# Attention scores issued one matmul ahead of each maximum, from the two auxiliary PSUM banks, instead of in alternating pairs over two kinds of banks

## The chip, the cores and the metric

The kernel runs on one core of a Trainium2 chip. The metric is the device time of one execution in microseconds (us); lower is better. One execution was also recorded by the hardware profiler, and all rows below come from that recording.

## The reference

Two layers of a decoder trunk over 256 tokens of width 1024. Each layer normalises, projects once, and feeds three mixers: sliding-window attention, a short gated convolution and a recurrent branch; then come a merge, a product-key expert FFN and a gated embedding. The part that matters here is the attention, 16 query heads over 4 key/value heads (a group of 4 query heads for each), 64 wide, in two blocks of 128 queries:

```python
scores = jnp.einsum('bnqhgd,bnkhd->bnhgqk', qb, kb,
                    preferred_element_type=jnp.float32) * (HEAD_DIM ** -0.5)
mask = (diff >= 0) & (diff < WINDOW) & (k_pos >= 0)
scores = jnp.where(mask[None, :, None, None], scores, NEG_INF)
m = jnp.maximum(scores.max(axis=-1, keepdims=True), sink)
e = jnp.exp(scores - m)
probs = e / (e.sum(axis=-1, keepdims=True) + jnp.exp(sink - m))
out = jnp.einsum('bnhgqk,bnkhd->bnqhgd', probs.astype(v.dtype), vb)
```

The first block of queries sees 128 keys, the second 256.

## The kernel before

Activations lie transposed, features on the partitions and the 256 tokens along the free axis. A weight is split into a rounded part and a rest (`split`, lines 152 to 161: ScalarE line 159, VectorE line 160), and each product is three matmuls, lines 184 to 186 in `pair`; 48 of them make one PSUM tile of two output chunks. Weights come as a stream, in the order of their use, and their loads and splits are issued ahead.

In a layer the projections of keys (`k`), queries (`q`) and values (`v`, lines 309 to 311) come first, then the attention (lines 315 to 370), then the convolution branch. That branch starts with three projections, `cx`, `cc` and `cb` (lines 375, 380, 388), 48 matmuls each. They need nothing from the attention, so the scheduler may put them between its instructions. Each engine works off its own list in order; the scheduler fixes that list when the kernel is built: of the instructions that it believes ready it takes the one that stands earliest in the program.

PSUM has three kinds of banks: four `acc`, two `mm` (projections, and half of the scores) and two `aux`.

The attention goes over block `b` (0 or 1) and pair of key/value heads `kt` (0 or 1). In a name such as `a01sc` the first digit is the block, the second the key/value head; `sc` is the score tile. The two heads of a pair lie on partitions 0 to 63 and 64 to 127, so a score matmul uses 64 rows of TensorE's array: the upper or the lower half. Steps:

1. Scores, line 328: for a whole pair of heads first, the two heads in turn, one head's tile in an `mm` bank, the other's in an `aux` bank. In block 0 a tile holds four groups of 128x128; in block 1 a head takes two tiles of two groups of 128x256.
2. Scale, mask and maximum in one VectorE operation for each group, line 343, from PSUM to the tile `e`; small operations on the maxima, lines 346 and 347.
3. Exponentials on ScalarE with their sums, lines 349 and 350; then VectorE divides, lines 351 to 354.
4. Four transposes on TensorE for each head and key block into an `acc` bank (`at`, line 361), copied by ScalarE (`et`, line 363), then the product with the values (`ao`, line 366): 64 columns of the array for each head, the left or the right half.
5. The result is split for the branch projection (`store`, lines 272 and 273).

Of the kernel before, what the change touches and what calls it, by code (L numbers as in the profile page):

```python
# [18 lines left out]
P = 128  # L19
# [79 lines left out]
def trunk_kernel(ctx: ExitStack, tc: tile.TileContext, xT, pT, vecs, wmix, wu, wv, outT, dbg=None, layers=NL):  # L99
    nc = tc.nc  # L100
# [12 lines left out]
    def acc_bank(name, shape=(P, 2, T)):  # L113
        return psum.tile(list(shape), F32, name=name, tag="acc", bufs=4)
# [4 lines left out]
    def aux_bank(name, shape=(P, 2, T)):  # L119
        return psum.tile(list(shape), F32, name=name, tag="aux", bufs=2)  # L120
# [149 lines left out]
    def store(dst, src, n=2):  # L270

        nc.scalar.copy(dst[0], src)
        nc.vector.tensor_sub(dst[1], src, dst[0].bitcast(F32))

    def new_big(name, dt=F32, shape=(P, KT, T)):
        return big.tile(list(shape), dt, name=name, tag="big")
# [4 lines left out]
    def t2(name, shape, dt=F32):  # L281
        return work.tile(list(shape), dt, name=name, tag="t2", bufs=3)
# [5 lines left out]
    def layer(l):  # L288
        V = l * V_LAYER
        st = Stream(l)  # L290
        L = "L%d" % l
# [3 lines left out]
        kT = work.tile([P, 2, T], F32, name=L + "kT", tag="wph")  # L295
        ps = pair(st, x1g, L + "k")
        nc.vector.tensor_mul(kT, ps, rb(r1))
        qT = new_big(L + "qT")
# [17 lines left out]
        for b in range(2):  # L316
            nk = b + 1
            for kt in range(2):
                ee = xp.tile([P, 2, 4, nk * P], F32, name=L + "e%d%d" % (b, kt), tag="x")

                scs = {}
                for half in range(nk):
                    for kv in range(2):
                        scs[kv, half] = (aux_bank if kv else mm_bank)(L + "a%d%dsc%d" % (b, 2 * kt + kv, half), (P, 4 // nk, nk * P))
                    for gg in range(4 // nk):
                        for kv in range(2):
                            r0 = kv * 64
                            nc.tensor.matmul(
                                scs[kv, half][:, gg, :], qT[r0 : r0 + 64, 4 * kt + half * 2 + gg, b * P : (b + 1) * P],
                                kT[r0 : r0 + 64, kt, 0 : nk * P], start=True, stop=True)  # L330
                for kv in (2 * kt, 2 * kt + 1):
                    n = L + "a%d%d" % (b, kv)
                    e = ee[:, kv % 2]
                    mx = small.tile([P, 4], F32, name=n + "m", tag="mx", bufs=4)
                    den = small.tile([P, 4], F32, name=n + "d", tag="den", bufs=4)
                    sk = small.tile([P, 4], F32, name=n + "s", tag="sk", bufs=4)

                    sinks = vec[:, V + V_SINK + 8 * kt : V + V_SINK + 8 * kt + 8].rearrange("p (g two) -> p g two", two=2)[:, :, kv % 2]
                    for half in range(nk):
                        sc = scs[kv % 2, half]  # L340
                        for gg in range(4 // nk):
                            g = half * 2 + gg
                            nc.vector.tensor_tensor_reduce(
                                e[:, g, :], sc[:, gg, :], mask.rearrange("p a k -> p (a k)")[:, (2 - nk) * P :],
                                0.125, sinks[:, g : g + 1], OP.add, OP.max, mx[:, g : g + 1])
                    nc.vector.tensor_sub(sk, sinks, mx)
                    nc.vector.tensor_scalar(mx, mx, -1.0, None, op0=OP.mult)
                    for g in range(4):
                        nc.scalar.activation(e[:, g, :], e[:, g, :], AF.Exp, bias=mx[:, g : g + 1], accum_out=den[:, g : g + 1])
                    nc.scalar.activation(sk, sk, AF.Exp)  # L350
                    nc.vector.tensor_add(den, den, sk)
                    nc.vector.reciprocal(den, den)
                    for g in range(4):
                        nc.vector.tensor_scalar(e[:, g, :], e[:, g, :], den[:, g : g + 1], None, op0=OP.mult)  # L354
                po = acc_bank(L + "ao%d%d" % (b, kt), (P, 4, P))
                for kb in range(nk):
                    ets = []
                    for kv in range(2):
                        pt = acc_bank(L + "at%d%d%d%d" % (b, kt, kv, kb), (P, 4, P))
                        for g in range(4):  # L360
                            nc.tensor.transpose(pt[:, g, :], ee[:, kv, g, kb * P : (kb + 1) * P], ident)  # L361
                        et = t2(L + "et%d%d%d%d" % (b, kt, kv, kb), (P, 4, P))
                        nc.scalar.copy(et, pt)  # L363
                        ets.append(et)
                    for kv in range(2):
                        nc.tensor.matmul(  # L366
                            po[kv * 64 : kv * 64 + 64, :, :], vt[:, kb, (2 * kt + kv) * 64 : (2 * kt + kv) * 64 + 64], ets[kv],
                            start=kb == 0, stop=kb == nk - 1, skip_group_check=True)
                s = slice(b * P, (b + 1) * P)
                store([a[:, 4 * kt : 4 * kt + 4, s] for a in attn], po)  # L370
# [83 lines left out]
        for n, branch in enumerate((attn, conv, rec)):  # L454
            for j in range(0, KT, 2):
                ps = pair(st, x1, L + "mg%d%d" % (n, j))
                g = work.tile([P, 2, T], F32, name=L + "gt%d%d" % (n, j), tag="w2a")
# [273 lines left out]
        for j in range(0, KT, 2):  # L731
            ps = pair(st, x3g, L + "pg%d" % j)
            g = work.tile([P, 2, T], F32, name=L + "pgs%d" % j, tag="w2a")
# [6 lines left out]
    for l in range(layers):  # L740
        layer(l)
# [66 lines left out]
```

## Time and profile before

| | |
|---|---|
| median of 3 runs | 2528.94 us (2527.0 to 2531.62) |
| profiled execution | 2527.01 us, its span 2525.3 us |
| TensorE (PE) busy | 2420.9 us, 96% of the span |
| VectorE (DVE) busy | 1779.0 us, 70% |
| ScalarE (ACT) busy | 1307.7 us, 52% |
| mean granted TensorE clock | 0.984 of full speed |

The span is what the profiler saw between the first and the last instruction; the time holds 1.7 us more around it. A matmul in float32 goes through the array in two passes, and the trace has one record for each pass. Records of neighbouring matmuls overlap, since one starts before the one ahead has drained: the distance between two starts tells the pace, the length of a record does not.

### The profile page before, as it was taken

How to read it: one execution, taken by the hardware profiler on the slowest of the kernel's cores; microseconds unless marked ns; L12 is line 12 of the kernel's file. 1: busy time of each engine (PE TensorE's matmuls, PEld its weight loads, DVE VectorE, ACT ScalarE, POOL GpSimd, SP SyncE). 2: the span in 40 equal slices, each digit the busy share in tenths (PEclk: the TensorE clock that was granted, in tenths of full speed). 3: DMA queues.
4: the chain of work that ended last, by engine and by line, in shares of the span. 5: the costliest groups of instructions: out<-in, count | busy, mean ns of one | idle time of the engine just before them, and what ended most of it. 6: DMA issues, size and time to landing. Idle time of an engine off the chain costs nothing. (4 is left out here: it accounts for less than half of the span.)

```text
span 2525.3 us, 42263 instructions
## 1 busy us (share of the span) xinstructions
PE 2420.9 (96%) x17336; PEld 2244.7 (89%) x17336; DVE 1779.0 (70%) x3100; ACT 1307.7 (52%) x1685; POOL 28.8 (1%) x44
## 2 busy tenths in 40 slices
PE   8999998979999999999999999989799999999997
PEld 7899998968899999988879999988798999999886
DVE  7666869999555555567776668699985555555666
ACT  5556454468444444444654554544674444444444
POOL 0000100000000000000000020000000000000000
PEclk9999999989999999999989999999899999999999
DMA  5355443447765656675424545534577566566752
GB/s 190 117 184 184 173 179 135 165 184 266 254 214 205 217 204 219 211 253 197 167 101 151 184 168 186 181 134 151 191 286 245 203 220 211 200 220 209 254 200 84
DMA packets 129459, 486.02 MB, mean 192 GB/s; under 512 B 7536, under 2 KB 73200, under 8 KB 74864
## 3 DMA queue, kind: packets, MB, share of 16 engines
q1 hardware_dynamic: 128976, 482.90, 54.5%
q8 instruction: 136, 2.23, 0.4%
q14 instruction: 59, 0.48, 0.1%
q10 hardware_dynamic: 288, 0.41, 0.0%
HBM read 448.67 MB, written 34.60 MB: 191 GB/s over the span
## 5 line engine op out<-in xcount | busy, mean ns | idle before, releaser
L663 DVE TENSOR_TENSOR L0wt<-L0act,L0gr 128x256 f32<-128x256 f32 x128 | 53.5, 422 | 3.0 <-DMA L0gr<-L0gd 1.0
L663 DVE TENSOR_TENSOR L1wt<-L1act,L1gr 128x256 f32<-128x256 f32 x128 | 53.5, 422 | 2.7 <-DMA L1gr<-L1gd 0.6
L652 ACT ACTIVATE L1act<-L1ua 128x512 f32<-128x512 f32 x64 | 38.0, 594 | 0.0
L652 ACT ACTIVATE L0act<-L0ua 128x512 f32<-128x512 f32 x64 | 38.0, 593 | 0.0
L488 PE MATMUL L0sc<-vec,L0pqs 128*128 128x128 f32 x64 | 9.5, 296 | 6.7 <-DVE L0pqs L505 6.7
L488 PE MATMUL L1sc<-vec,L1pqs 128*128 128x128 f32 x64 | 9.5, 296 | 6.6 <-DVE L1pqs L505 6.6
L488 PEld LDWEIGHTS L0sc<-vec,L0pqs 128*128 128x128 f32 x64 | 8.6, 209 | 7.0 <-issue 7.0
L488 PEld LDWEIGHTS L1sc<-vec,L1pqs 128*128 128x128 f32 x64 | 8.6, 209 | 7.0 <-issue 7.0
L438 DVE RECIPROCAL L0ru<-L0ru 128x256 f32<-128x256 f32 x8 | 14.0, 1746 | 0.1
L438 DVE RECIPROCAL L1ru<-L1ru 128x256 f32<-128x256 f32 x8 | 14.0, 1744 | 0.1
L379 POOL MEMSET L1pc<- 128x4 f32 x4 | 0.4, 103 | 1133.8 <-DVE L1cy L387 1122.4
L366 PE MATMUL L1ao<-L1et,L1vt 128*64 128x512 f32 x24 | 12.4, 770 | 0.1
L361 PEld LDWEIGHTS L1at<-ident,L1e 128*128 128x128 f32 x48 | 6.6, 167 | 6.5 <-DVE L1e L354 1.8
L366 PE MATMUL L0ao<-L0et,L0vt 128*64 128x512 f32 x24 | 11.0, 657 | 0.1
L361 PEld LDWEIGHTS L0at<-ident,L0e 128*128 128x128 f32 x48 | 6.0, 153 | 5.3 <-DVE L0e L354 1.8
L408 DVE SCALAR_TENSOR_TENSOR L1xr<-L1pr,vec,L1xr 128x256 f32<-128x256 f32 x24 | 10.3, 481 | 0.0
L408 DVE SCALAR_TENSOR_TENSOR L0xr<-L0pr,vec,L0xr 128x256 f32<-128x256 f32 x24 | 10.3, 480 | 0.0
L184 PE MATMUL L0k<-L0n1gh,w_0h 128*128 128x256 f32 x8 | 3.3, 412 | 7.2 <-ACT w_0h L159 7.2
L628 PE MATMUL L1t1pg<-L1t1og 128*128 128x128 f16 x16 | 2.0, 307 | 8.3 <-DVE L1t1og L613 8.3
L628 PE MATMUL L0t1pg<-L0t1og 128*128 128x128 f16 x16 | 2.0, 309 | 8.3 <-DVE L0t1og L613 8.3
L363 ACT COPY L1et<-L1at 128x512 f32<-128x512 f32 x12 | 6.7, 582 | 6.3 <-PE L1at L361 6.3
L361 PE MATMUL L1at<-ident,L1e 128*128 128x128 f32 x48 | 9.8, 331 | 0.0
(7266 smaller groups left out, 10950.2 us busy)
## 6 DMA issues: line engine op xcount, KB each, us to landing
w<-wmix SPq DMA_DIRECT2D x137, 1024.0 KB, 4.8
L0u<-wu SPq DMA_DIRECT2D x64, 1024.0 KB, 5.0
L0v<-wv SPq DMA_DIRECT2D x64, 1024.0 KB, 4.8
L1u<-wu SPq DMA_DIRECT2D x64, 1024.0 KB, 4.9
L1v<-wv SPq DMA_DIRECT2D x64, 1024.0 KB, 4.8
L0gr<-L0gd SPq DMA_DIRECT2D x16, 1024.0 KB, 5.9
L1gr<-L1gd SPq DMA_DIRECT2D x16, 1024.0 KB, 5.9
L0gd<-L0t0st SPq DMA_DIRECT2D x1, 1024.0 KB, 4.8
```

What stands on the lines that cost most here:

```text
L184: nc.tensor.matmul(out, w[0], xh, start=start, stop=False, **kw)
L361: nc.tensor.transpose(pt[:, g, :], ee[:, kv, g, kb * P : (kb + 1) * P], ident)
L363: nc.scalar.copy(et, pt)
L366: nc.tensor.matmul(po[kv * 64 : kv * 64 + 64, :, :], vt[:, kb, (2 * kt + kv) * 64 : (2 * kt + kv) * 64 + 64], ets[kv], start=kb == 0, stop ...
L379: nc.gpsimd.memset(pc[:, :, 0:2], 0.0)
L408: nc.vector.scalar_tensor_tensor(o, pr[:, c, i : i + T], w[i], o, op0=OP.mult, op1=OP.add)
L438: nc.vector.reciprocal(u[:, c, :], u[:, c, :])
L488: nc.tensor.matmul(sp[:, b, a, :], q[:, a, b * P : (b + 1) * P], keys[:, a, :], start=True, stop=True)
L628: nc.tensor.matmul(pg[:, t, :], oh[:, 2, t4 + t, :], oh[:, i, t4 + t, :], start=i == 0, stop=i == 1)
L652: nc.scalar.activation(acts[i // 4][:, i % 4 * 2 : i % 4 * 2 + 2, :], ps, AF.Gelu_apprx_tanh)
L663: nc.vector.tensor_mul(wt[:, e, :].rearrange("p (g t) -> p g t", t=SG), acts[i // 4][:, o + e, :].rearrange("p (g t) -> p g t", t=SG), gre ...
```

## The change

The block that issued all scores of a pair of heads ahead of the loop over heads is gone. Each score matmul is now written directly before the VectorE operation that reads it, and all score tiles come from the two `aux` banks. Everything behind line 345 is the same, seven lines higher (the maximum stands in line 336, transposes in 354, the product with the values in 359).

```diff
                 ee = xp.tile([P, 2, 4, nk * P], F32, name=L + "e%d%d" % (b, kt), tag="x")
-
-                scs = {}
-                for half in range(nk):
-                    for kv in range(2):
-                        scs[kv, half] = (aux_bank if kv else mm_bank)(L + "a%d%dsc%d" % (b, 2 * kt + kv, half), (P, 4 // nk, nk * P))
-                    for gg in range(4 // nk):
-                        for kv in range(2):
-                            r0 = kv * 64
-                            nc.tensor.matmul(
-                                scs[kv, half][:, gg, :], qT[r0 : r0 + 64, 4 * kt + half * 2 + gg, b * P : (b + 1) * P],
-                                kT[r0 : r0 + 64, kt, 0 : nk * P], start=True, stop=True)
                 for kv in (2 * kt, 2 * kt + 1):
...
                     for half in range(nk):
-                        sc = scs[kv % 2, half]
+                        sc = aux_bank(n + "sc%d" % half, (P, 4 // nk, nk * P))
+                        r0 = kv % 2 * 64
                         for gg in range(4 // nk):
                             g = half * 2 + gg
+                            nc.tensor.matmul(
+                                sc[:, gg, :], qT[r0 : r0 + 64, 4 * kt + g, b * P : (b + 1) * P],
+                                kT[r0 : r0 + 64, kt, 0 : nk * P], start=True, stop=True)
                             nc.vector.tensor_tensor_reduce(
```

The built program holds the same matmuls, transposes and VectorE and ScalarE operations in the same numbers, and outside the stretch from the first score to the end of `cb`, in both layers, every engine has the same list as before. Inside it the lists differ. TensorE in layer 0, from the last matmul of the values on, in the kernel before:

```order
L311 MATMUL L0v<-w_11h,L0n1sl 128x256
L328 MATMUL L0a00sc_549<-L0kT,L0qT 128x128
L328 MATMUL L0a01sc_550<-L0kT,L0qT 128x128
L328 MATMUL L0a00sc_549<-L0kT,L0qT 128x128
L328 MATMUL L0a01sc_550<-L0kT,L0qT 128x128
L328 MATMUL L0a00sc_549<-L0kT,L0qT 128x128
L328 MATMUL L0a01sc_550<-L0kT,L0qT 128x128
```

The same place in the changed kernel:

```order
L311 MATMUL L0v<-w_11h,L0n1sl 128x256
L333 MATMUL L0a00sc_552<-L0kT,L0qT 128x128
L333 MATMUL L0a01sc_577<-L0kT,L0qT 128x128
L184 MATMUL L0cx_866<-L0n1sh,w_12h 128x256
L185 MATMUL L0cx_866<-L0n1sl,w_12h 128x256
L186 MATMUL L0cx_866<-L0n1sh,w_12l 128x256
L333 MATMUL L0a00sc_552<-L0kT,L0qT 128x128
L184 MATMUL L0cx_866<-L0n1sh,w_12h 128x256
L333 MATMUL L0a01sc_577<-L0kT,L0qT 128x128
L185 MATMUL L0cx_866<-L0n1sl,w_12h 128x256
L186 MATMUL L0cx_866<-L0n1sh,w_12l 128x256
L333 MATMUL L0a00sc_552<-L0kT,L0qT 128x128
```

The 16 scores of block 0 stood in one unbroken run, the heads in turn; now all but the first two stand alone, with one to eleven `cx` matmuls between them, 31 in all before the last score of block 0.

Further on TensorE in layer 0, where block 0's first product with the values stands, in the kernel before:

```order
L361 MATMUL L0at_607<-ident,L0e_548 128x128 x4
L366 MATMUL L0ao_599<-L0et_605,L0vt 64x512
L366 MATMUL L0ao_599<-L0et_612,L0vt 64x512
L328 MATMUL L0a12sc_777<-L0kT,L0qT 128x256 x2
L328 MATMUL L0a12sc_783<-L0kT,L0qT 128x256 x2
L328 MATMUL L0a13sc_778<-L0kT,L0qT 128x256
```

and in the changed kernel, with the scores of block 1 (`a10`, `a11`) about it:

```order
L359 MATMUL L0ao_599<-L0et_605,L0vt 64x512
L354 MATMUL L0at_607<-ident,L0e_548 128x128
L185 MATMUL L0cx_866<-L0n1sl,w_13h 128x256
...
L184 MATMUL L0cc_929<-L0n1sh,w_14h 128x256
L333 MATMUL L0a10sc_692<-L0kT,L0qT 128x256
L359 MATMUL L0ao_599<-L0et_612,L0vt 64x512
L185 MATMUL L0cc_929<-L0n1sl,w_14h 128x256
L333 MATMUL L0a10sc_697<-L0kT,L0qT 128x256
L354 MATMUL L0at_670<-ident,L0e_618 128x128 x4
L186 MATMUL L0cc_929<-L0n1sh,w_14l 128x256
L184 MATMUL L0cc_929<-L0n1sh,w_14h 128x256
L333 MATMUL L0a11sc_718<-L0kT,L0qT 128x256
```

The two halves of the first `ao` were neighbours and are apart. The 16 scores of block 1 stood in 6 stretches in a layer, the first of them right behind block 0's run, and stand in 13. Along the whole list of a layer, the part of the array that TensorE uses (all of it, half the rows for a score, half the columns for an `ao`) changed 25 times and changes 71 times, each change between two neighbouring matmuls.

VectorE in layer 0, where the first division of `e` stands in the changed kernel (line 347, which was line 354):

```order
L336 ISA L0e_618,L0a03m<-L0a03sc_647,mask,vec 128x128
L336 ISA L0a03m 128x1
L344 TENSOR_TENSOR L0a00d<-L0a00d,L0a00s 128x4
L340 TENSOR_SCALAR L0a02m<-L0a02m 128x4
L339 TENSOR_TENSOR L0a03s<-vec,L0a03m 128x4
L345 RECIPROCAL L0a00d<-L0a00d 128x4
L340 TENSOR_SCALAR L0a03m<-L0a03m 128x4
L347 TENSOR_SCALAR L0e_548<-L0e_548,L0a00d 128x128 x4
```

As before, it stands behind the last maximum of head 3 (`a03`), so it follows the last score of block 0.

## Rows read from the trace of the kernel before

**Rows 1.** The page's head: the span, and what TensorE was busy of it.
```profile
span 2525.3 us, 42263 instructions
PE 2420.9 (96%) x17336; PEld 2244.7 (89%) x17336; DVE 1779.0 (70%) x3100; ACT 1307.7 (52%) x1685; POOL 28.8 (1%) x44
```

**Rows 2.** Busy time by stretch; columns named in the first row.
```profile
core 0: us, PE busy (x) PEld busy (x) DVE busy (x) ACT busy (x) POOL busy (x), PEclk, DMA share, GB/s
46.06:97.20 51.14, 48.32 (x283) 33.54 (x281) 34.65 (x145) 32.36 (x97) 0.10 (x1) 0.93 0.18 62
1294.30:1348.64 54.34, 51.72 (x283) 35.66 (x282) 34.76 (x145) 32.47 (x97) 0.10 (x1) 0.84 0.16 59
52.88:59.70 6.82, 6.82 (x19) 3.91 (x19) 4.47 (x29) 3.88 (x18) 0.00 (x0) 0.50 0.01 2
1298.74:1308.98 10.24, 10.24 (x28) 5.94 (x26) 7.29 (x49) 6.11 (x28) 0.00 (x0) 0.50 0.01 2
1312.40:1319.22 6.82, 6.82 (x17) 3.20 (x18) 4.18 (x22) 3.12 (x12) 0.00 (x0) 0.50 0.00 0
```

**Rows 3.** Timeline of PE, block 0's scores: start, length, line, out<-in, idle before.
```profile
45.94 0.28 PE L311 MATMUL L0v<-w_11h,L0n1sl 128*128 128x256 f32 x1
46.15 0.37 PE L328 MATMUL L0a00sc<-L0kT,L0qT 64*128 64x128 f32 x1
46.16 0.37 PE L328 MATMUL L0a01sc<-L0kT,L0qT 64*128 64x128 f32 x1
...
47.82 0.27 PE L328 MATMUL L0a02sc<-L0kT,L0qT 64*128 64x128 f32 x1
...
47.93 0.27 PE L328 MATMUL L0a02sc<-L0kT,L0qT 64*128 64x128 f32 x1
...
50.19 0.48 PE L328 MATMUL L0a10sc<-L0kT,L0qT 64*128 64x256 f32 x1 [1.98 <-DVE L0a00m L343]
```

**Rows 4.** Timeline of PE, block 1's scores: in a run, and alone.
```profile
60.35 0.48 PE L328 MATMUL L0a12sc<-L0kT,L0qT 64*128 64x256 f32 x1
...
60.35 1.99 PE L328 MATMUL L0a12sc<-L0kT,L0qT 64*128 64x256 f32 x8
...
62.91 0.48 PE L328 MATMUL L0a13sc<-L0kT,L0qT 64*128 64x256 f32 x1 [0.56 <-DVE L0a11m L343]
...
67.93 0.38 PE L361 MATMUL L0at<-ident,L0e 128*128 128x128 f32 x2
68.25 0.70 PE L328 MATMUL L0a13sc<-L0kT,L0qT 64*128 64x256 f32 x2
68.87 0.39 PE L184 MATMUL L0cx<-L0n1sh,w_12h 128*128 128x256 f32 x1
69.09 0.28 PE L185 MATMUL L0cx<-L0n1sl,w_12h 128*128 128x256 f32 x1
```

**Rows 5.** Timeline of PE, products with the values between projections.
```profile
72.17 1.07 PE L366 MATMUL L0ao<-L0et,L0vt 128*64 128x512 f32 x2
...
76.11 0.28 PE L186 MATMUL L0cx<-L0n1sh,w_13l 128*128 128x256 f32 x1
76.31 1.08 PE L366 MATMUL L0ao<-L0et,L0vt 128*64 128x512 f32 x4
77.32 0.38 PE L184 MATMUL L0cx<-L0n1sh,w_13h 128*128 128x256 f32 x1
77.55 0.28 PE L185 MATMUL L0cx<-L0n1sl,w_13h 128*128 128x256 f32 x1
```

**Rows 6.** Timeline of PE, one transpose between projections.
```profile
78.62 0.28 PE L185 MATMUL L0cx<-L0n1sl,w_13h 128*128 128x256 f32 x1
78.74 0.27 PE L361 MATMUL L0at<-ident,L0e 128*128 128x128 f32 x1
...
78.97 0.28 PE L184 MATMUL L0cx<-L0n1sh,w_13h 128*128 128x256 f32 x1
```

**Rows 7.** Timeline of DVE: the first maximum and the first division.
```profile
48.97 0.34 DVE L343 CUSTOM_DVE_ANT_0 L0e<-L0a00sc,mask,vec 128x128 f32<-128x128 f32 x1
...
54.02 0.87 DVE L354 TENSOR_SCALAR L0e<-L0e,L0a00d 128x128 f32<-128x128 f32 x4
```

## Prediction, written before the changed kernel was run

> **What bounds the kernel now.** I read the head of the page first: TensorE (PE) is busy 96% of the span [rows 1], so time is PE work plus the few stretches in which PE waits or runs slowly. Then the busy time by stretch around the change. From the end of the values to the end of `cb` a layer takes 51.1 us in layer 0 and 54.3 us in layer 1 [rows 2]. The lists of the two layers are alike there; what differs is the clock, granted at 0.93 and 0.84. The last three of those rows show it: at 0.50 of full speed, the lower level of 1.2 GHz, for 6.8 us in layer 0 and for 10.2 + 6.8 us in layer 1. Ahead of the first fall PE had been waiting: 1.98 us, until VectorE had read the first score tile [rows 3]. Another wait for VectorE is 0.56 us [rows 4]. Behind `cb` both versions have one list, and PE is busy throughout there, so what PE gains or loses in these two stages the whole kernel gains or loses, as long as PE remains what ends them.
>
> The stage's 144 projection matmuls, at a start every 0.12 us (78.62 to 78.74) [rows 6], take 17.3 us in both versions. What changes is the price of scores and of products with the values (`ao`), the waits and the clock.
>
> **The change, part by part.** All for one layer and at the full clock, unless said.
>
> *The price of standing alone.* A score uses half the rows of the array, an `ao` half the columns. In a run, passes over 256 columns start every 0.216 us: eight records span 1.99 us, one 0.48 us, and 1.51 over seven steps is 0.216 [rows 4]. A score on its own is dearer. The transpose ahead, which in its run starts 0.11 us after its neighbour (0.38 less 0.27), starts at 68.04 and the score at 68.25, 0.10 late; the two passes take 0.62 us to the next start instead of 0.43, 0.19 late; the next matmul needs 0.22 us instead of 0.12, 0.10 late [rows 4]. Together 0.39 us. An `ao` between projections shows the same: 0.20 instead of 0.12 us ahead of it, 1.01 us where two passes over 512 columns are 0.86 (an estimate, four times 0.216), then 0.23 instead of 0.12 [rows 5]. Together 0.34 us. A transpose between projections, on the whole array, shows no such price: 0.35 us from one projection to the next but one, that is 0.24 and its own 0.11 [rows 6]. I take 0.38 us for each insertion, with 0.34 and 0.39 as the measured ends. A score of 128 columns alone between projections isn't in the trace; its start is: 0.21 us after the matmul ahead instead of 0.12 [rows 3]. Its unknown end I bound by nothing and by 0.39.
>
> The Trainium skill, TensorEngine Tiling (Array Packing), Key Properties, has a rule that speaks against this change: changing the tiling mode, rather than only the tile, drains TensorE, while different tiles of one mode run in parallel. The transpose without a price and the score and the `ao` with one agree with it [rows 4 to 6]; the page gives no figure. By the rule every added change of mode is paid for; if it were only a first score after a wait that is dear, the added insertions would be nearly free and the sum below would come out at 2517 us.
>
> *Block 0's scores.* Before, heads in turn: two heads start 0.01 us apart and a pass follows every 0.11 us for both [rows 3], so 16 scores of two passes take 16 x 0.11 = 1.76 us. After, only the first two stand together (three steps of 0.11 = 0.33 us) and 14 stand alone, 2 x 0.11 = 0.22 us each: 3.08 + 0.33 = 3.41. That is +1.65 us for the lost overlap, and 14 more insertions.
>
> *Block 1's scores.* They overlap nowhere in either list to speak of; six stretches, the first with no switch ahead of it, become 13: 8 more insertions.
>
> *The first `ao`.* Two neighbours run side by side: four passes last 1.08 us [rows 5], two last 1.07. Apart they cost two passes more, 0.86 us, and one more insertion.
>
> So 14 + 8 + 1 = 23 more insertions, which is also what 71 instead of 25 changes of array part give at two an insertion: 23 x 0.38 = 8.7 us. With the lost overlap, 8.7 + 1.65 + 0.86 = **+11.2 us**.
>
> *Waits that go.* The 1.98 us ahead of `a10` and the 0.56 us ahead of `a13` [rows 3, 4] are filled by projections: **-2.5 us**.
>
> *Waits that come.* Each score of block 0 now waits until VectorE has read the score two places before it in that bank. A maximum takes 0.34 us [rows 7]; PE comes back to a bank after two scores of 0.22 + 0.38 and about four projections of 0.12, 1.7 us. So VectorE is done first, and these waits cost nothing. What is queued behind them are the projections. The first division comes later, though: block 0's scores now last 3.41 + 15 x 0.38 + 31 x 0.12 = 12.8 us, so the last is read at about 46.1 + 12.8 + 0.7 = 59.6 (0.37 for the pass to drain [rows 3], 0.34 for the maximum), and the division starts there instead of at 54.0 [rows 7]. Transposes, exponentials of block 1 and the later `ao` slide by some 5.6 us, and who waits is PE. The cover is the 113 projections that are still to come, 13.6 us, spread between the late pieces up to the last `ao`. I take that this hides it, which costs nothing; if the cover were gone it costs up to 5.6 us in each layer.
>
> *The queues.* No DMA is issued within the moved lines. In the stage the weights' loads and splits keep their order, DMA is at 0.16 to 0.18 of its share [rows 2]; I cost that at nothing.
>
> *The clock.* Without the wait of 1.98 us the falls may go. In layer 0 that is worth 6.8 us at half speed, -3.4 us. In layer 1 the 10.2 us more of low clock cost only the 3.2 us by which its stage is longer, since PE waited for others in part of it: 3.4 + 3.2, -6.6 us. Against it: the scores keep half the array busy, and the drained steps none of it, for a stretch of nearly 13 us. Layer 1 fell a second time, at 1312.4 [rows 2], with the same list with which layer 0 kept its clock at that place. I count one low stretch of 6.8 us as likely as not in each layer, so one in the two: +3.4 us, with none and two of layer 1's size in each as the ends.
>
> **Sum.** Layer 0: 11.2 - 2.5 - 3.4 = +5.3. Layer 1: 11.2 - 2.5 - 6.6 = +2.1. With +3.4 for the clock, +10.8 us. On the profiled execution, 2527.01 (its span of 2525.3 and 1.7 around it), that is 2537.8; the median of the runs shown, 2528.94, lies 1.9 higher, which would give 2539.7. I say 2538.
>
> **Rivals.**
>
> *The cover wins (faster).* Insertions cost little between projections, because the next weights are loaded while the last matmul runs. Then the two layers pay 2 x 2.5 us for lost overlap and gain 5.0 us of waits and 10.0 us of low clock: -10, so 2517. For it: PE does have filler now where it stood for 1.98 us. Against it: the isolated score and the isolated `ao`, both beside projections, were dear. It decides from the price of an insertion: 46 x price = 15 - 5 = 10, so below 0.22 us the change is faster. Chance 0.16.
>
> *It evens out.* With a price between 0.11 and 0.33 us and no low clock the sum is within 5 us of before: about 2529. For it: the unknown end of a 128-column score; if only its start of 0.2 us is dear, 14 of the 23 insertions cost half. Chance 0.20.
>
> *The clock stays low (slower still).* Layer 1's 17.1 us of low clock in both layers, now all of it on PE: 8.5 us each, 7.4 + 17 = +24, 2551; a first division 5.6 us late without cover in each layer, 7.4 + 11.2, would give 2546. Chance 0.12.
>
> That the change doesn't do what it says would need the scheduler to leave the pairs together; its list doesn't, so that holds no chance of its own.
>
> **Chances and range.** The forecast holds 0.52; its own range is 2533 (price of 0.34, full clock) to 2546 (two low stretches and some lost cover). Before can be told from after from 0.2%, 5.1 us: below 2523.9 or above 2534.0. Slower 0.52 + 0.12 = 0.64, same 0.20, faster 0.16. The range for 8 in 10 reaches into the even case and just past it, and part of the way to the low clock: 2522 to 2548.
>
> **What would show it.** In the profile after: block 0's 16 scores spread over about 13 us with 31 `cx` matmuls among them, each alone and 0.4 us dearer than its two passes; no idle time of PE ahead of `a10`; the first division near 59.6 us; the stage of layer 0 at 55 to 57 us and of layer 1 about the same, where before they differed by 3.2; the clock at 1.00 in one of them at least. The prediction is wrong if a lone score costs 0.3 us or less beyond its passes, if PE stands waiting in the second half of the stage, or if anything behind `cb` moves.

## The result, and the profile after

The changed kernel is slower: 2540.07 us, the median of 7 runs (2537.59 to 2552.29), beside 2528.07 us for the kernel before in 7 runs on the same chip (2523.73 to 2531.62). The ratio is 1.0051, with a 95% interval of 1.0038 to 1.0064, so the loss, half a per cent, can be told from none. The forecast was 2538 us. Medians leave out executions in the chip's slower state, two of the 15 of before beside e5.

The profiled execution's span is 2535.9 us, 10.6 longer than before's. The page's head, as in [rows 1]:

```profile
span 2535.9 us, 42242 instructions
PE 2436.9 (96%) x17336; PEld 2251.9 (89%) x17336; DVE 1779.9 (70%) x3100; ACT 1307.1 (52%) x1685; POOL 28.8 (1%) x44
```

The matmuls are the same in number and PE was busy with them for 16 us longer, while the span grew by 10.6: waits became busy time. The busy time by stretch shows where, with the columns of [rows 2]. The first two rows are the two layers' stages from the end of the values to the end of `cb`, the third is the only stretch of low clock in them:

```profile
46.13:105.16 59.03, 58.93 (x283) 38.54 (x282) 34.78 (x144) 32.96 (x98) 0.10 (x1) 0.91 0.20 72
1304.70:1359.16 54.46, 54.38 (x282) 35.20 (x281) 34.77 (x144) 32.95 (x98) 0.13 (x1) 1.00 0.22 78
56.63:66.87 10.24, 10.24 (x34) 7.83 (x34) 3.96 (x25) 2.99 (x16) 0.00 (x0) 0.50 0.00 0
```

Against [rows 2], layer 0 pays 7.9 us and layer 1 0.1. PE has 0.1 us of idle time left in each, where it had 2.8 and 2.6. Layer 1 now runs at the full clock throughout, which before did in neither layer's stage. What is left of the 10.6 us, 2.5, arises in layer 0's expert stage, on unchanged lists, where the clock is also at its lower level for longer: 23.9 us in place of 20.5.

The timeline of PE in layer 0, block 0's scores (start, length, line, out<-in), beside [rows 3]:

```profile
46.22 0.37 PE L333 MATMUL L0a00sc<-L0kT,L0qT 64*128 64x128 f32 x1
46.22 0.37 PE L333 MATMUL L0a01sc<-L0kT,L0qT 64*128 64x128 f32 x1
...
48.64 0.28 PE L186 MATMUL L0cx<-L0n1sh,w_12l 128*128 128x256 f32 x1
48.85 0.49 PE L333 MATMUL L0a00sc<-L0kT,L0qT 64*128 64x128 f32 x2
49.26 0.38 PE L184 MATMUL L0cx<-L0n1sh,w_12h 128*128 128x256 f32 x1
49.58 0.48 PE L333 MATMUL L0a01sc<-L0kT,L0qT 64*128 64x128 f32 x2
49.99 0.38 PE L185 MATMUL L0cx<-L0n1sl,w_12h 128*128 128x256 f32 x1
50.22 0.28 PE L186 MATMUL L0cx<-L0n1sh,w_12l 128*128 128x256 f32 x1
...
59.84 0.79 PE L333 MATMUL L0a03sc<-L0kT,L0qT 64*128 64x128 f32 x2
...
78.83 0.48 PE L333 MATMUL L0a12sc<-L0kT,L0qT 64*128 64x256 f32 x1
78.83 0.48 PE L333 MATMUL L0a11sc<-L0kT,L0qT 64*128 64x256 f32 x1
79.15 0.38 PE L333 MATMUL L0a12sc<-L0kT,L0qT 64*128 64x256 f32 x1
79.15 0.38 PE L333 MATMUL L0a11sc<-L0kT,L0qT 64*128 64x256 f32 x1
```

The first two scores still run side by side (46.22 twice). A lone one is read from starts: from the score at 48.85 to the next at 49.58 are 0.73 us, for one score and one projection. At a pace of 0.12 us for the projection and 2 x 0.11 for the two passes, 0.39 us belong to neither. PE counts as busy in them. The last four rows are two scores of block 1 that happen to stand side by side: four passes in the time of two.

In layer 1, at the full clock, block 0's scores run from the first start at 1304.79 to that of `a10` at 1317.74, 13.0 us:

```profile
1304.79 0.37 PE L333 MATMUL L1a00sc<-L1kT,L1qT 64*128 64x128 f32 x1
...
1317.74 1.13 PE L333 MATMUL L1a10sc<-L1kT,L1qT 64*128 64x256 f32 x4
```

Passes and projections make 7.25 of these 12.95 us (the scores' 3.41 us of the prediction, and 32 x 0.12, one of them behind the last score); the rest, over the 15 places where scores stand, is 0.38 us each. So the lone score above is no exception. VectorE's first division of layer 0, the answer to [rows 7]:

```profile
61.37 0.87 DVE L347 TENSOR_SCALAR L0e<-L0e,L0a00d 128x128 f32<-128x128 f32 x4
```

### The profile page after: what moved, and what is told of

It is laid out like the page before. It is cut to its first block, busy times and chain, and to the rows that moved or that the text cites. A ratio compares the mean times of both kernels' runs of the same rounds, so it can differ in the third digit from the quotient of the medians.

```text
span 2535.9 us, 42242 instructions
## 1 busy us (share of the span) xinstructions
PE 2436.9 (96%) x17336; PEld 2251.9 (89%) x17336; DVE 1779.9 (70%) x3100; ACT 1307.1 (52%) x1685; POOL 28.8 (1%) x44
## 5 line engine op out<-in xcount | busy, mean ns | idle before, releaser
L356 ACT COPY L0et<-L0at 128x512 f32<-128x512 f32 x12 | 6.7, 587 | 10.2 <-PE L0at L354 10.2
L356 ACT COPY L1et<-L1at 128x512 f32<-128x512 f32 x12 | 6.7, 587 | 7.3 <-PE L1at L354 7.3
L401 DVE SCALAR_TENSOR_TENSOR L1xr<-L1pr,vec,L1xr 128x256 f32<-128x256 f32 x24 | 10.3, 480 | 0.0
L401 DVE SCALAR_TENSOR_TENSOR L0xr<-L0pr,vec,L0xr 128x256 f32<-128x256 f32 x24 | 10.3, 480 | 0.0
L354 PEld LDWEIGHTS L0at<-ident,L0e 128*128 128x128 f32 x48 | 6.0, 148 | 4.2 <-issue 2.6
```

Source lines behind the costliest of these rows:

```text
L401: nc.vector.scalar_tensor_tensor(o, pr[:, c, i : i + T], w[i], o, op0=OP.mult, op1=OP.add)
```

## Experiments

Nine runs were made: seven edited kernels, and both kernels once more. Theory: a lone score between projections costs what the two changes of the array part cost, 0.39 us. Rivals: what costs is the lost overlap of the two heads; or the waits behind the two banks; or the clock. Stages are compared over a longer stretch, from the first matmul of the values to the first of the merge gate, since every list agrees again there. For before it is, by stretch, layer 0 then layer 1:

```profile
40.30:195.10 154.80, 151.98 (x1146) 137.16 (x1145) 104.05 (x238) 84.34 (x159) 0.73 (x7) 0.98 0.41 143
1288.50:1446.60 158.10, 155.48 (x1147) 139.38 (x1146) 104.21 (x238) 84.45 (x159) 0.73 (x7) 0.95 0.40 140
```

The same for after:

```profile
40.40:203.10 162.70, 162.60 (x1147) 142.16 (x1146) 104.71 (x238) 84.42 (x159) 0.73 (x7) 0.97 0.38 136
1298.90:1457.10 158.20, 158.12 (x1147) 138.90 (x1146) 104.70 (x238) 84.41 (x159) 0.76 (x7) 1.00 0.39 140
```

Low clock in these: 6.8 and 17.1 us before, 10.2 and none after.

**Only the order of the code (e1_mixed_banks).** The new order, with the old two kinds of banks:

```diff
-                        sc = aux_bank(n + "sc%d" % half, (P, 4 // nk, nk * P))
+                        sc = (aux_bank if kv % 2 else mm_bank)(n + "sc%d" % half, (P, 4 // nk, nk * P))
```

Expected:

> The changed kernel with one edit: the score tiles of even heads come from the projections' two banks again, those of odd heads from the auxiliary ones, as in the kernel before; each score still stands directly ahead of its maximum in the code. The list then has no projection among block 0's scores and 27 changes of array part in a layer, before 25, the changed kernel 71. Theory (lone scores among projections pay 0.39 us each for the change of array part, and it is the free projection bank that puts projections there): as before, 2526 to 2531 us, with the idle time ahead of block 1's scores and the low clock back. Rival (it is the writing of each score ahead of its maximum that costs, by VectorE's read standing between two scores): 2536 us or more.

Measured: 2536.52 us, ratio 1.003 [1.0016, 1.0045]. The part on the list came true: with an `mm` bank held by scores no projection stands between block 0's scores. The total missed. PE's waits are back; waits of PE in layer 1's stage (who waits for whom: us in total, times, longest):

```profile
PE L1a03sc L333 <- DVE L1a03m L336: 1.5, 2, 1.1
PE L1a13sc L333 <- DVE L1a11m L336: 0.7, 1, 0.7
PE L1a10sc L333 <- DVE L1a10m L336: 0.6, 1, 0.6
PE L1a11sc L333 <- DVE L1a03m L336: 0.5, 1, 0.5
```

The stages were 162.3 us (20.5 of it at the low clock) and 156.7 (3.4 of it). So the projections between the scores come from the freed `mm` bank, not from the code order. The order by itself is no gain either: the total met the rival's 2536 us, since scores then wait for VectorE with nothing to fill the wait, and layer 0 ran 20.5 us at the low clock.

**The same list, without a change of array part (e2_full_rows).** Keys are stored twice, with zeros in the other head's rows, and each score uses all 128 rows; the list of PE is that of after.

```diff
-        kT = work.tile([P, 2, T], F32, name=L + "kT", tag="wph")
         ps = pair(st, x1g, L + "k")
-        nc.vector.tensor_mul(kT, ps, rb(r1))
+        kz = work.tile([P, 2, 2, T], F32, name=L + "kz", tag="kz", bufs=1)
+        nc.gpsimd.memset(kz, 0.0)
+        for kv in range(2):
+            nc.vector.tensor_mul(kz[kv * 64 : kv * 64 + 64, kv], ps[kv * 64 : kv * 64 + 64], rb(r1)[kv * 64 : kv * 64 + 64])
...
-                                sc[:, gg, :], qT[r0 : r0 + 64, 4 * kt + g, b * P : (b + 1) * P],
-                                kT[r0 : r0 + 64, kt, 0 : nk * P], start=True, stop=True)
+                                sc[:, gg, :], qT[:, 4 * kt + g, b * P : (b + 1) * P],
+                                kz[:, kv % 2, kt, 0 : nk * P], start=True, stop=True)
```

Expected:

> The changed kernel with the same list on every engine but for the keys: they are stored twice, each time with the rows of the other head at zero, so that a score uses all 128 rows of the array with the queries of both heads, and gives the same numbers. A score then isn't another array part than a projection. Theory (the change of array part costs 0.19 us each): 28 lone scores in a layer cost 0.38 less, 10 us less in a layer, and the 5 us of low clock in layer 0 may go: 2515 to 2522 us, faster than before. Rival (the loss is the overlap of the two heads, 5 us, and the low clock, 5 us, and a lone score costs no more than its passes): overlap isn't given back, so 2535 to 2541 us. In the trace a score of 128 columns between projections should take 0.22 us by the theory, 0.61 by the rival.

Measured: the timeline of PE between the first score and the first of block 1, with a place of the same kind as above at 51.41,

```profile
47.78 0.39 PE L334 MATMUL L0a00sc<-L0kz,L0qT 128*128 128x128 f32 x2
...
49.40 0.28 PE L186 MATMUL L0cx<-L0n1sh,w_12l 128*128 128x256 f32 x1
49.55 0.49 PE L334 MATMUL L0a00sc<-L0kz,L0qT 128*128 128x128 f32 x2
49.80 0.37 PE L184 MATMUL L0cx<-L0n1sh,w_12h 128*128 128x256 f32 x1
50.00 0.38 PE L334 MATMUL L0a01sc<-L0kz,L0qT 128*128 128x128 f32 x2
...
51.41 0.38 PE L334 MATMUL L0a00sc<-L0kz,L0qT 128*128 128x128 f32 x2
51.55 0.36 PE L186 MATMUL L0cx<-L0n1sh,w_12l 128*128 128x256 f32 x1
51.75 0.38 PE L334 MATMUL L0a01sc<-L0kz,L0qT 128*128 128x128 f32 x2
...
56.00 1.17 PE L334 MATMUL L0a10sc<-L0kz,L0qT 128*128 128x256 f32 x4
```

and by stretch the two stages, and layer 0 from the first sums of its expert stage (`acc`) to the keys of layer 1:

```profile
42.00:191.90 149.90, 149.82 (x1147) 138.03 (x1146) 104.32 (x238) 84.35 (x159) 1.69 (x8) 1.00 0.42 148
1298.40:1448.30 149.90, 149.82 (x1146) 138.04 (x1145) 104.33 (x238) 84.35 (x159) 0.77 (x7) 1.00 0.41 148
649.20:1265.60 616.40, 614.83 (x3655) 545.11 (x3656) 366.58 (x435) 295.30 (x350) 0.00 (x0) 0.99 0.61 209
```

From the score at 51.41 to the next 0.34 us, that is 0.12 + 0.22 and nothing more. Other scores keep a part of the price: from 49.40 to 50.00 are 0.60 us for one score and two projections, 0.14 more than 0.22 + 0.24. On average over block 0, 8.22 us (47.78 to 56.00) for 16 x 0.22 + 32 x 0.12 = 7.36, it is 0.05 us a score, where after pays 0.38. What this rest is stays open. The stage falls from after's 158.2, at the same full clock, to 149.9. That is 8.3 us, where 10 were expected: beside the rest, 0.9 us in block 0, two overlaps that after still has (46.22 and 78.83 above; 0.22 + 0.43 us) are gone. This is the experiment that settles the price: same order, same banks, same neighbours. The total did not show it: 2533.57 us, ratio 1.0011 [1.0002, 1.0019], because both expert stages, with unchanged lists, came out some 9 us longer (616.4 where before has 607.0; the last section shows what took longer).

**Full rows in the order of before (e3_full_rows_before).** The same keys and scores in before's code: no overlap of heads anywhere, and no price.

```diff
-                                scs[kv, half][:, gg, :], qT[r0 : r0 + 64, 4 * kt + half * 2 + gg, b * P : (b + 1) * P],
-                                kT[r0 : r0 + 64, kt, 0 : nk * P], start=True, stop=True)
+                                scs[kv, half][:, gg, :], qT[:, 4 * kt + half * 2 + gg, b * P : (b + 1) * P],
+                                kz[:, kv, kt, 0 : nk * P], start=True, stop=True)
```

Expected:

> The kernel before with the keys stored twice with zeros, scores over all 128 rows; list as before. It takes the overlap of the two heads alone, and the few changes of array part at the scores. Theory: block 0's scores last 3.5 us instead of 1.8, but the wait for VectorE behind them is as much shorter, since VectorE begins with the first head's tile after it is free of the weight split; 9 changes of array part fewer give 1.7 us in a layer: 2524 to 2528 us, with the idle time ahead of block 1 near 0.3 us. Rival (overlap is what the changed kernel lost): 2531 to 2534 us.

Measured: 152.1 us in both stages, no low clock, PE waiting 1.3 us of it. That is shorter than either of before's, though every overlap is lost; and against what before's stage would be at the full clock (151.4 to 152.6 us by the estimates further down) it is longer by 0.7 us at most. That is a net: the list has nine changes of array part fewer, some 1.7 us by the price, and PE waits 1.3 us in place of 2.6. So by this estimate the lost overlap costs 3.7 us at most, with every overlap gone. After still has some of them and has its waits filled, and yet by the same estimates its stage lies 5.6 to 6.8 us above before's at the full clock: the lost overlap isn't the loss of after by itself. The total, 2536.96 us and 1.0029 [1.0018, 1.004], carries longer expert stages again.

**Runs of one head and half, all in `aux` banks (e4_runs_aux).** The new banks without the lone scores: for each half, the scores of both heads are issued in turn, then all their maxima.

```diff
+                for half in range(nk):
+                    scs = [aux_bank(L + "a%d%dsc%d" % (b, 2 * kt + kv, half), (P, 4 // nk, nk * P)) for kv in range(2)]
+                    for gg in range(4 // nk):
+                        for kv in range(2):
+                            r0 = kv * 64
+                            nc.tensor.matmul(
+                                scs[kv][:, gg, :], qT[r0 : r0 + 64, 4 * kt + half * 2 + gg, b * P : (b + 1) * P],
+                                kT[r0 : r0 + 64, kt, 0 : nk * P], start=True, stop=True)
+                    for kv in range(2):
+                        for gg in range(4 // nk):
...
```

Expected:

> All score tiles from the auxiliary banks as in the changed kernel, but the code issues the scores of both heads' tiles together, in turn, and then their maxima. Block 0's first 8 scores are one run with overlap, then runs of four and, in block 1, of two; 43 changes of array part in a layer instead of 71, projections between the runs. Theory: 28 fewer changes at 0.19 and 0.9 us of overlap are 6 us less in a layer than in the changed kernel, of which 0.9 goes for one more pair of products with the values standing apart: 2526 to 2530 us, and some 4 us less where layer 0 keeps the full clock. Rival (the auxiliary banks alone are the cost, since a head's tile waits for the one before): 2536 us or more, with PE idle ahead of scores.

Measured: 2525.02 us, ratio 0.9986 [0.9977, 0.9995]. The array part changes 43 times in a layer, between before's 25 and after's 71. Layer 0's stage, at the full clock:

```profile
41.30:194.60 153.30, 152.61 (x1146) 136.62 (x1145) 103.56 (x238) 84.33 (x159) 0.73 (x7) 1.00 0.41 145
```

It is 4.9 us shorter than after's at the full clock, with waits of 0.3 us twice; layer 1's is 153.4. So freeing the `mm` bank is worth having as long as the scores stay in runs.

**Full rows with the keys in their old place (e5_full_rows_in_place).** As e2, but the two copies lie in the tile that held the keys and in a small tile that is free at that time; the zeros go to the unused halves alone.

```diff
+        kz = [work.tile([P, 2, T], F32, name=L + "kT", tag="wph"), small.tile([P, 2, T], F32, name=L + "kU", tag="eT", bufs=2)]
+        for kv in range(2):
+            r = slice(kv * 64, kv * 64 + 64)
+            nc.gpsimd.memset(kz[kv][64 - kv * 64 : 128 - kv * 64], 0.0)
+            nc.vector.tensor_mul(kz[kv][r], ps[r], rb(r1)[r])
```

Expected:

> Full-row scores in the changed kernel's order once more, but the two zero-filled copies of the keys lie where the keys and a tile of the later expert stage lay, so that no tile of the kernel moves in SBUF. In the run with full rows before, the attention stages were shorter by 12.8 and 8.3 us than the changed kernel's, yet each expert stage, whose lists are the same, was some 9 us longer. If that came from where the tiles lie, this one keeps the gain: stages of 150 us from the values to the merge against 158 and 163, and 2514 to 2520 us in all, against some 2529 before. If the longer expert stages come from something else in full-row scores, it stays at 2531 to 2537 us.

Measured: 2519.54 us, ratio 0.9959 [0.9944, 0.9973]. It beats both kernels: 11.9 us below before's median in that comparison, 2531.44, and 23.4 below after's there (2542.91, in e7). PE's timeline:

```profile
48.08 0.36 PE L184 MATMUL L0cx<-L0n1sh,w_12h 128*128 128x256 f32 x1
48.28 0.38 PE L335 MATMUL L0a01sc<-L0kU,L0qT 128*128 128x128 f32 x2
48.42 0.36 PE L185 MATMUL L0cx<-L0n1sl,w_12h 128*128 128x256 f32 x1
```

The two stages, and the expert stretch of layer 0 as in e2:

```profile
41.20:191.10 149.90, 149.82 (x1146) 138.02 (x1145) 104.32 (x238) 84.30 (x159) 0.73 (x7) 1.00 0.41 148
1286.50:1436.40 149.90, 149.83 (x1147) 138.03 (x1146) 104.33 (x238) 84.29 (x159) 0.73 (x7) 1.00 0.41 148
646.30:1253.70 607.40, 605.84 (x3656) 543.13 (x3656) 366.12 (x434) 294.90 (x350) 0.52 (x1) 1.00 0.61 212
```

A projection follows 0.14 us behind the score's start (48.28, 48.42), and the next projection 0.20 later: 0.34 for a projection and two passes, as in e2. The expert stretch is back at before's length, so the whole gain of the stages reaches the total.

**A spare tile (e6_spare_tile).** Why were e2's expert stages longer? Before's code with an unused tile of the size of e2's keys:

```diff
+        spare = work.tile([P, 2, 2, T], F32, name=L + "spare", tag="spare", bufs=1)
+        nc.gpsimd.memset(spare, 0.0)
```

Expected:

> The kernel before with one more tile of 4 KB a partition, set to zero on GpSimd and never read, in the pool where the two copies of the keys lay; nothing else changed. If the place of tiles in SBUF made the expert stages of the full-row runs longer, this kernel is slower than before by 10 to 18 us, all of it in the expert stages. If not, it is within 4 us of before.

Measured: 2530.54 us, ratio 0.9997 [0.9986, 1.0007], expert stretch 607.4 us. Shifting the tiles behind it is not the cause by itself. Its stages were 155.5 and 155.2 us, with 10.2 us of low clock in each.

**After once more (e7_after_again).** No edit. Expected:

> The changed kernel as it is, for a second profile beside the same runs of before. Theory: the attention stages at the full clock repeat to 0.3 us (158.2 us from the values to the merge, 59 less 5.1 of clock in layer 0), while the low stretches fall elsewhere: layer 0 or 1 may have one of 3 to 10 us or none. Rival (the low stretch in layer 0 belongs to the list): it is there again with about 10 us in layer 0 and none in layer 1.

Measured: 2542.91 us, ratio 1.0052 [1.0036, 1.0068]. The two stages:

```profile
40.40:203.10 162.70, 162.60 (x1147) 142.18 (x1146) 104.72 (x238) 84.64 (x159) 0.73 (x7) 0.97 0.39 136
1298.90:1461.60 162.70, 162.62 (x1146) 141.84 (x1145) 104.67 (x238) 84.64 (x159) 0.76 (x7) 0.97 0.38 137
```

Layer 0 repeats to the tenth. Layer 1, which ran in 158.2 us at the full clock, now has 10.2 us of low clock too, and takes 162.7. So neither expectation held in full: the low stretch of layer 0 was there again, and layer 1 had one as well. The two profiles of one kernel so give the price of such a stretch here: 4.5 us.

**Before once more (e8_before_again).** No edit. Expected:

> The kernel before as it is, for a second profile. Theory: low clock again in both attention stages, since PE stands for 2 us in each, of 7 to 17 us; the stages last 151 us plus half of the low clock or a little less.

Measured: 2530.93 us; the stages are 154.9 and 158.1 us, with 6.8 and 17.1 us of low clock, as in the first profile.

**Keys and values exchanged (e9_swap_places).** Before's code, with the two tiles' places exchanged:

```diff
-        kT = work.tile([P, 2, T], F32, name=L + "kT", tag="wph")
+        kT = work.tile([P, 2, T], F32, name=L + "kT", tag="wpl")
...
-        vt = work.tile([P, 2, 256], F32, name=L + "vt", tag="wpl")
+        vt = work.tile([P, 2, 256], F32, name=L + "vt", tag="wph")
```

Expected:

> The kernel before with the keys and the values exchanging their tiles' places (one line each); lists and sizes are the same. In the full-row runs whose keys had left their place the expert stages, with unchanged lists, took about 9 us longer; the run with a spare tile did not, nor did the full-row run in which the keys kept their place. If it is the order in which the places of the expert stage's two product tiles are laid out that counts, this kernel is 10 to 18 us slower than before, in the expert stages; if not, it is within 4 us of before and the cause of those 9 us stays open.

Measured: 2528.78 us, ratio 0.9997 [0.9987, 1.0006], expert stretch 607.3 us. The keys' place alone isn't the cause of e2's longer expert stages either.

## Why the prediction was right, and where its sizes were off

**The price of standing alone: right.** Forecast 0.38 us for each insertion; a lone score measured 0.39 us, and 0.05 on average (0.00 at one place, 0.14 at another) when the same scores in the same places use the whole array. The bound that was unknown, a 128-column score alone between projections, lies at its upper end. Of the Trainium skill the rule weighed in the prediction (TensorEngine Tiling (Array Packing), Key Properties) is borne out: these runs show a price of 0.38 us on average where the array part changes, and 0.05 where it doesn't. The same page of the Trainium skill, in its Overview, recommends reconfiguring the array into smaller tiles where the contracted dimension is 64 or less. Here that pays only where two such matmuls are neighbours (46.22 twice): for a lone one, e2 and e5 show the whole array cheaper, 0.22 to 0.36 us for a score instead of 0.61.

**Waits that go: right.** The 2.0 and 0.6 us ahead of `a10` and `a13` are gone in both layers, and by e1 it is the free bank that lets projections fill them.

**Waits that come: right at nothing.** PE has no wait in the stages of after, though the first division came at 61.4 us, later than the 59.6 that were forecast; the low clock from 56.6 on reaches into block 0's last scores. The 113 projections still covered it. In layer 1, at the full clock, block 0's scores took 13.0 us, forecast 12.8, and the first division came 13.4 us behind the first score's start (1318.23), forecast 13.5.

**The sum at the full clock: too large.** After has a measured full-clock stage, 158.2 us. That is 3.4 and 0.1 us above before's two stages, 154.8 and 158.1 with their low clock, where the prediction's sums without new low clock are 5.3 and 2.1: 3.5 us in both layers instead of 7.4. Against a full clock on both sides the change can't be read alike: before never ran at it there, so its stage has to be estimated. Taking half of layer 0's low clock off, as the prediction did, it is 154.8 - 3.4 = 151.4, which makes the difference 6.8 us, not 11.2 - 2.5 = 8.7. One part of that is shown: `a12` and `a11` overlap in block 1 (78.83 twice), two passes of 0.216 us saved, 0.43 us, where the prediction had no overlap. The rest, 1.5 us, stays open. If a low stretch cost before less than half its length, the gap is wider still: its two stages differ by 3.3 us for 10.3 us more of low clock, and at that rate the full-clock stage would be 152.6, the difference 5.6. The rate isn't steady: e6's two stages of the same list, with 10.2 us of low clock each, took 155.5 and 155.2.

**The clock: the size was off.** The old low stretches went, as forecast. The new one was counted as 6.8 us in one layer of the two, 3.4 us in all. It came as 10.2 us in layer 0, in both profiles, and in layer 1 in one of two; each costs 4.5 us. So layer 0 lost more than forecast, 7.9 instead of 5.3 with half of the +3.4 on top, 7.0, and layer 1 in the first profile less, 0.1 instead of 2.1 + 1.7 = 3.8. The low clock in layer 0 begins at 56.6 us, with PE busy throughout and without a wait ahead of it, in the middle of the lone scores. With full rows (e2, e5) the four stages had none.

**Where the total still came out.** The stages gave 7.9 + 0.1 = 8.0 us instead of 10.8. Only 3.5 of the 8.0 are there with after at the full clock; 4.5 are the low stretch of layer 0. 2.5 us more came from layer 0's expert stage, which the prediction had at nothing. Its lists are unchanged, and low clock in it is 3.4 us longer than before's. In the second profiles the difference, from the merge gate to the first sums, is there again: 456.7 us in e7, 454.9 in e8. So it went with the changed kernel both times, but no run shows how the change would bring it about. In e7 the stages alone gave 7.9 + 4.6 = 12.5 us. The nearness of 2540 to 2538 is thus in good part luck: a sum at the full clock that was 3.9 us too large, and a low clock and an expert stage that cost more than forecast. The direction isn't luck: without most of the price, e2's stages are shorter than before's, and with it, at the full clock, after's are not.

**The rivals.** *The cover wins* needed a price below 0.22 us: measured 0.39. *It evens out* asked for 128-column scores cheaper than the others, and they are not. Its sum came nearer than its price: at the full clock in both layers the stages cost 3.5 us, within its 5 us. What carries the total beyond that is the low clock and layer 0's expert stage. *The clock stays low* came true in part, at 4.5 us a stretch instead of 8.5, and without the division's wait. Of the forecast's own signs two failed in layer 0 by its low clock: the stages at 55 to 57 us and nearly equal were 59.0 and 54.5, and the first division came at 61.4. And work behind `cb` did move, by the 2.5 us above, which the prediction itself named as a sign of being wrong.

## What to carry to other kernels

Before work is slipped between matmuls to fill a wait, count how often the list then goes from the whole array to a part of it and back, and price each such lone matmul from starts in the trace; here 0.39 us, more in sum than the waits that were filled. Narrow matmuls belong in runs, or side by side on different parts of the array. Where they must stand alone, padding the operand that is already stored with zeros to the full rows takes most of the price away, and then the filling pays: the same order, with full rows, is the fastest version here.

## What the runs showed that was not expected

Storing the keys in a tile of their own (e2, e3) made both expert stages longer, with unchanged lists: 616.4 and 613.5 us in layer 0 instead of 607.0. An unused tile of that size (607.4), exchanged places of keys and values (607.3) and full rows with the keys in their old place (607.4) did not. What took longer can be read. The `acc` matmuls alone in that stretch, before and e3 (columns as in [rows 2], without POOL):

```profile
649.40:1256.40 607.00, 355.88 (x1536) 285.73 (x1536) 1.38 (x2) 1.17 (x2) 1.00 0.62 212
649.50:1263.00 613.50, 362.55 (x1536) 285.53 (x1536) 1.38 (x2) 1.16 (x2) 1.00 0.61 210
```

At the same full clock these 1536 matmuls keep PE busy 6.7 us longer, some 4 ns each, and that accounts for the whole difference of e3, 6.5. In e2 another 2.9 us come with 6.8 us of low clock; the same amount of it costs before 2.8 in e8 (609.8). Why the matmuls are slower, and what in the place of the tiles decides it, stays open.

PE's granted clock fell to its lower level (0.50, 1.2 GHz) in a stretch in which PE was busy without a gap. What it did ahead were scores on half of the array between projections; the same list with full rows kept 1.00 in four stages of four. The changed kernel's own list kept 1.00 in one stage of four, so the list alone doesn't decide it, and the cause stays open.
